# The affine part of three layer norms moved from GpSimd to VectorE, and scheduler priority round four groups of chains

## The chip, the cores and the metric

One core of one Trainium2 chip runs the whole program. A core has five engines that run beside each other, each with its own queue of instructions in program order: TensorE (PE, matrix products; PEld is its weight load), VectorE (DVE), ScalarE (ACT), GpSimd (POOL) and SyncE (SP, which here only issues DMAs). An instruction waits on semaphores until what it reads is written and what it overwrites has been read; everything behind it in the same queue waits with it. The metric is the device time of one execution in microseconds (us). Times of small kernels are written in us throughout, durations of one instruction sometimes in ns.

## The reference, cut to what matters

The reference is one step of a small diffusion backbone of two layers, for 384 tokens (128 of a context, 256 of a sample) of width 1024. Each layer has a mixing part (an mLSTM, a convolution and a retention branch, merged by gates) and a feed-forward part, and each part ends in a residual and a layer norm:

```python
def trunk_layer(x, mod, p, init, latent):
    shift1, scale1, gate1, shift2, scale2, gate2 = jnp.split(mod[:, None, :], 6, axis=-1)
    h = x * (1.0 + scale1) + shift1
    mix, new_state = mixing_sublayer(h, p, init, latent)
    x = layer_norm(DEEPNORM_ALPHA * x + gate1 * mix, p['ln1_w'], p['ln1_b'])
    h = x * (1.0 + scale2) + shift2
    a, gt = jnp.split(h @ p['ffn_w13'], 2, axis=-1)
    ff = (jax.nn.silu(gt) * a) @ p['ffn_w2']
    x = layer_norm(DEEPNORM_ALPHA * x + gate2 * ff, p['ln2_w'], p['ln2_b'])
    return x, new_state
```

The norm is `(x - mu) * rsqrt(var + eps) * w + b`. Its last two steps, times `w` and plus `b`, are called the affine part here. The next product reads `h`, a scaled and shifted norm; the affine result itself is read only by the residual after that.

## The kernel before, in words

**Products.** Everything is in fp32, and a product is made of three passes: each operand is split into a high part (a cast) and a low part (the rest), and PE adds high x high (L255), high x low and low x high (L256, L257). Weights come by DMA on SP's queue into three buffers (`wraw`), ACT casts the high part (`whi`, L205, five buffers) and DVE subtracts for the low part (`wlo`, L206, four buffers). So every weight tile passes through SP, ACT and DVE in this order before PE can use it. Activations are split likewise (`h1h`, `h1l` before a mixing part, `h2h`, `h2l` before a feed-forward part, `fAh`, `fAl` within it).

**Tokens.** The 384 tokens lie in three tiles `x0`, `x1`, `x2` of 128 tokens by 1024. A projection (`proj`) takes the output columns in two halves of 512 and the tokens t = 0, 1, 2 within each half. After each product DVE scales it by the gate (L423, `gmix`), adds it to `x` (L425 or L427) and takes statistics (L431). Behind the second half of a token stands the norm: statistics merged (L436), variance plus epsilon (`rs_ve`, L318, DVE), its power -1/2 on POOL (`rs`, L319), and `x` minus the mean times `rs` on DVE (L442, in two halves).

**From the norm to the next product.** `make_hT` transposes a token's `x` on PE (L306, two groups of four), ACT applies scale and shift with the norm's weights already folded in (`hf`, L310), DVE casts the high part (L313) and subtracts the low part (L314). It is called for token t once token t + 1 has been normed; the last call is held back into the first product of the next stage, which begins with token 0, then 1, then 2. Behind each `make_hT` stands `affine`: on POOL, in place in `x`, times `w` (L450) and plus `b` (L451), two halves each. This happens at three places: norm 1 of layer 0, norm 2 of layer 0, norm 1 of layer 1. The last norm of all works with the weights at once (L444, L445) and has no `affine`. The prediction calls the three places C, D and E; they lie at 456 to 485, 761 to 796 and 1186 to 1220 us of the span.

**What sets the order.** The code is written in the order of the products; helpers that run beside them are Python generators on a list, and `tick()` after each product advances each of them by a step (`spawn(gen, delay)` waits `delay` ticks first; `finish` runs one to its end). The mLSTM and retention heads, the gates, the convolution's taps (`cacc`, L756) and the loading of later modulation constants go this way. A scheduler then orders the instructions of each engine by dependencies, priorities and the order of the program; the queues of the trace are its result.

**Retention heads.** A head makes decay weights (`gef`), two score products, then DVE multiplies scores by decay: `rpa` (L705, L706) and `rpb` (L707), which PE reads at once in L710 and L714. `rgT` (L771) is a gate of the same branch: a product times a sigmoid `sig` from ACT (L770).

**Constants of the norms.** `ln_consts` (L414) issues eight DMAs on SP that spread gate, weight and bias rows over 128 partitions into `lnc`; they share a pool of buffers with other tiles, and SP waits in its queue where a buffer is still read.

Of the kernel before, what the change touches and what calls it, by code (L numbers as in the profile page):

```python
# [14 lines left out]
P = 128  # L15
# [25 lines left out]
        (1, 3): ((1, 3, 0, 16),), (1, 5): ((0, 3),)}  # L41
WHI = 5
# [55 lines left out]
def tile_kernel(ctx: ExitStack, tc: tile.TileContext, a: dict, o: list):  # L98
# [37 lines left out]
    rate = {"fill": 0.0, "acc": 0.0, "taps": 0.0, "tacc": 0.0}  # L136

# [161 lines left out]
    def make_hT(ha, t, S, B):  # L299

        m = 0 if t == 0 else 1
        for q in range(2):
            ps = psum()
            for j in range(4):
                f = 4 * q + j
                tr(ps[:, j * P:(j + 1) * P], x[t][:, f * P:(f + 1) * P], ident)  # L306
            hf = tmp((P, 4, P), "hf")
            for j in range(4):
                f = 4 * q + j
                act(hf[:, j, :], ps[:, j * P:(j + 1) * P], AF.Identity, bias=B[:, f, m:m + 1], scale=S[:, f, m:m + 1])  # L310
            h, l_ = ha.t[q]
            s = slice(t * P, (t + 1) * P)
            nc.vector.tensor_copy(h[:, :, s], hf)  # L313
            tt(l_[:, :, s], hf, h[:, :, s].bitcast(F32), op=ALU.subtract)  # L314
# [179 lines left out]
    def mixing(l, ha, v1, rv):  # L494
# [26 lines left out]
        def gates(ps):  # L521
# [8 lines left out]
            nc.vector.tensor_copy(natG, pt[:, 0:48].rearrange("p (t c) -> p t c", c=16))  # L530
            gv = natG.rearrange("p t (d g h) -> p t d g h", d=2, g=2)
            X = tmp((P, NT, 2, NH), "X", 1)
            nc.vector.tensor_copy(X, gv[:, :, :, 1, :])
            lf = tmp((P, NT, 2, NH), "lf", 1)
            log_sigmoid(lf.rearrange("p t d h -> p (t d h)"), X.rearrange("p t d h -> p (t d h)"), (P, 24))
            for d in range(2):
                c0 = 32 * d
                nc.vector.tensor_copy(GG[:, :, 0, c0:c0 + 4], gv[:, :, d, 0, :])
                ts_(GG[:, :, 1 + d, c0:c0 + 4], lf[:, :, d, :], -1.0, None, op0=ALU.mult)
                nc.vector.tensor_copy(GG[:, :, 1 + d, c0 + 4:c0 + 8], lf[:, :, d, :])  # L540
# [8 lines left out]
            nc.vector.tensor_copy(R, pr[:, 0:T])  # L549
            scan = nc.vector.tensor_tensor_scan  # L550
            scan(R[64:68, 0:P], R[0:4, 0:P], R[0:4, 0:P], 0.0, op0=ALU.max, op1=ALU.max)
            scan(R[64:68, P:T], R[0:4, P:T], R[0:4, P:T], m0r[0:4, :], op0=ALU.max, op1=ALU.max)
            rp = slice(P - 1, None, -1)
            rs_ = slice(T - 1, P - 1, -1)
            scan(R[96:100, rp], R[32:36, rp], R[32:36, rp], 0.0, op0=ALU.max, op1=ALU.max)
            scan(R[96:100, rs_], R[32:36, rs_], R[32:36, rs_], m0r[32:36, :], op0=ALU.max, op1=ALU.max)
            act(RM[64:128, :], R[64:128, :], AF.Copy, scale=-1.0)
            stt(RM[0:64, :], R[64:128, :], -1.0, RM[64:128, :].bitcast(F32), op0=ALU.mult, op1=ALU.subtract)
# [4 lines left out]
            nc.vector.tensor_copy(natR, pn[:, 0:T].rearrange("p (t c) -> p t c", c=P))  # L563
            rb = natR.rearrange("p t (s d c) -> p t s d c", s=2, d=2)
            tt(nm, rb[:, :, 0, :, 4:8], rb[:, :, 1, :, 0:4], op=ALU.add)
            act(enm, nm, AF.Exp, scale=-1.0)
# [30 lines left out]
        def mheads():  # L597
# [3 lines left out]
            for h in range(NH):  # L601
                b1, b2 = scores(mkT, mqT, h)
                pts, qws, kws = [], [], []
                for d in range(2):
# [4 lines left out]
                    win = tmp((P, 256), "win")  # L609
                    act(win, pm[:, P:T], AF.Exp, bias=m0b[:, d, h:h + 1])  # L610
                    dl = tmp((P, 512), "dl")
                    if d == 0:
                        segs = ((0, P, 0, 0, MF[:, 0:P]), (P, 256, P, 1, MF), (T, P, 256, 2, MF[:, 0:P]))
                    else:
                        segs = ((0, P, 0, 0, MB[:, P:256]), (P, P, P, 1, MB[:, P:256]), (256, 256, P, 2, MB))
                    for o0, n, i0, t, msk in segs:
                        stt(dl[:, o0:o0 + n], pm[:, i0:i0 + n], av[:, t:t + 1], msk, op0=ALU.add, op1=ALU.min)
                    act(dl, dl, AF.Exp)
                    kw = tmp((P, P), "kw")
                    wcol = dl[:, 127:128] if d == 0 else dl[:, 0:1]  # L620
                    act(kw, kn[:, h, :], AF.Copy, scale=wcol)
                    qw = tmp((P, 256), "qw")
                    nc.gpsimd.tensor_tensor(qw, mqT[:, h, P:T], win, op=ALU.mult)
                    if d == 0:
# [450 lines left out]
    for l in range(DEPTH):  # L1075
        mA = mixing(l, ha, v1, rv)
        while l == 0 and len(fillers) > 27:
            fill()
# [4 lines left out]
        def after1(t):  # L1083
            make_hT(h2, t, S2, B2)
            affine(t, lc)
# [59 lines left out]
```

## Time and profile before

| | |
|---|---|
| median of 3 runs | 1487.69 us (1487.66, 1487.69, 1488.17) |
| the profiled execution | 1490.92 us, span of its instructions 1488.9 us |
| PE busy | 1438.7 us, 97% of the span |
| DVE busy | 944.7 us, 63% |
| ACT busy | 576.8 us, 39% |
| POOL busy | 233.2 us, 16% |
| mean granted TensorE clock | 0.984 of full speed |

The profile counts a matmul as busy from issue to its modelled end, so 97% says that PE has nearly always something in hand, not that it streams at its peak. The span is from the first to the last instruction; 2.0 us of the profiled execution lie outside it, and that execution is 3.2 us above the median of the runs without a profile. In the rows below a number in square brackets is idle time of that engine just before the instruction, with the work that ended it.

### The profile page before, as it was taken

What the parts mean: (1) busy time and instruction counts of PE and PEld (TensorE: products, weight loads), DVE (VectorE), ACT (ScalarE), POOL (GpSimd) and SP (SyncE); (2) the same over time, 40 slices, a digit from 0 to 9 for tenths busy, and PEclk for the clock granted to TensorE, in tenths of its full rate; (3) what the DMA queues carried; (4) which work ended last, traced back from release to release, by engine and by line L of the source; (5) the groups of instructions that cost most, each with busy time, mean ns of one, the idle gap of its engine ahead of it and who ended that gap; (6) DMA issues with size and microseconds to landing.
All of it is one profiled execution on the core that took longest, in us unless ns stands there. A gap on an engine that the chain in (4) does not pass through costs nothing. (4 is left out here: it accounts for less than half of the span.)

```text
span 1488.9 us, 20492 instructions
## 1 busy us (share of the span) xinstructions
PE 1438.7 (97%) x7990; PEld 1302.5 (87%) x7990; DVE 944.7 (63%) x1755; ACT 576.8 (39%) x1026; POOL 233.2 (16%) x242
## 2 busy tenths in 40 slices
PE   6999999999998999999999999989999989999997
PEld 4799999989986888979967999989999869899996
DVE  3457688996647545354375477989975674454446
ACT  2434555332523423323243345553325243242330
POOL 1003233002214100000042023320021250000000
PEclk8999999999999999999999999999999999999999
DMA  9465352464473474645644532324434525243441
GB/s 330 159 226 173 125 185 87 154 226 158 138 259 128 142 254 131 222 155 173 212 141 122 162 118 81 118 68 124 132 108 147 169 71 202 82 155 100 142 156 42
DMA packets 131713, 226.22 MB, mean 152 GB/s; under 512 B 12552, under 2 KB 62200, under 8 KB 126496
## 3 DMA queue, kind: packets, MB, share of 16 engines
q1 hardware_dynamic: 130144, 222.78, 45.2%
q0 software_dynamic: 1472, 2.14, 0.5%
q8 instruction: 62, 1.02, 0.3%
q14 instruction: 35, 0.29, 0.1%
HBM read 221.18 MB, written 3.71 MB: 151 GB/s over the span
## 5 line engine op out<-in xcount | busy, mean ns | idle before, releaser
L205 ACT CAST whi<-wraw 128x512 fp32r<-128x512 f32 (+1 forms) x484 | 338.7, 722 | 624.5 <-PE ps L256 268.1
L206 DVE TENSOR_TENSOR wlo<-wraw,whi 128x512 fp32r<-128x512 f32 (+1 forms) x484 | 403.5, 857 | 195.4 <-PE ps L257 92.4
L255 PE MATMUL ps<-h1h,whi 128*128 128x384 f32 x896 | 306.0, 341 | 0.0
L257 PE MATMUL ps<-h1h,wlo 128*128 128x384 f32 x896 | 299.9, 335 | 0.0
L256 PE MATMUL ps<-h1l,whi 128*128 128x384 f32 x896 | 299.8, 335 | 0.0
L255 PE MATMUL ps<-h2h,whi 128*128 128x384 f32 x576 | 193.9, 337 | 0.0
L257 PE MATMUL ps<-h2h,wlo 128*128 128x384 f32 x576 | 192.6, 334 | 0.0
L256 PE MATMUL ps<-h2l,whi 128*128 128x384 f32 x576 | 192.6, 334 | 0.0
L255 PEld LDWEIGHTS ps<-h1h,whi 128*128 128x128 f32 x896 | 168.4, 188 | 13.7 <-issue 8.4
L256 PEld LDWEIGHTS ps<-h1l,whi 128*128 128x128 f32 x896 | 168.5, 188 | 0.1
L257 PEld LDWEIGHTS ps<-h1h,wlo 128*128 128x128 f32 x896 | 168.3, 188 | 0.0
L756 DVE SCALAR_TENSOR_TENSOR cacc<-u,cwt,cacc 128x399 f32<-128x399 f32 x232 | 148.6, 661 | 2.0
L255 PEld LDWEIGHTS ps<-h2h,whi 128*128 128x128 f32 x576 | 108.1, 188 | 8.5 <-issue 4.2
L256 PEld LDWEIGHTS ps<-h2l,whi 128*128 128x128 f32 x576 | 108.1, 188 | 0.2
L257 PEld LDWEIGHTS ps<-h2h,wlo 128*128 128x128 f32 x576 | 108.1, 188 | 0.0
L255 PE MATMUL ps<-whi,fAh 128*128 128x512 f32 x264 | 103.4, 392 | 0.0
L257 PE MATMUL ps<-whi,fAl 128*128 128x512 f32 x264 | 102.9, 390 | 0.0
L256 PE MATMUL ps<-wlo,fAh 128*128 128x512 f32 x264 | 102.8, 389 | 0.0
L423 DVE TENSOR_TENSOR gmix<-ps,lnc 128x512 f32<-128x512 f32 x48 | 33.1, 689 | 81.2 <-PE ps L257 81.2
L928 DVE TENSOR_TENSOR gf<-ps,sig 128x384 f32<-128x384 f32 x36 | 20.1, 558 | 91.1 <-PE ps L257 91.1
L319 POOL TENSOR_TENSOR rs<-rs_ve,half 128x1 f32<-128x1 f32 x18 | 15.4, 856 | 380.8 <-DVE rs_ve L318 380.8
L844 POOL TENSOR_TENSOR mg<-mg,sig 128x384 f32<-128x384 f32 x32 | 42.4, 1330 | 200.5 <-DVE sig L843 200.5
(303 smaller groups left out, 2194.8 us busy)
## 6 DMA issues: line engine op xcount, KB each, us to landing
wraw<-in_in_w_dram SPq DMA_DIRECT2D x64, 1024.0 KB
wada<-in_ada_w_dram SPq DMA_DIRECT2D x40, 1024.0 KB
wraw<-in_ffn_w_dram SPq DMA_DIRECT2D x76, 512.0 KB
wraw<-in_ffn_w_dram SPq DMA_DIRECT2D x28, 1024.0 KB
wraw<-in_out_w_dram SPq DMA_DIRECT2D x8, 1024.0 KB
adaq<-in_ada_w_dram SPq DMA_DIRECT2D x8, 512.0 KB
wraw<-in_mlstm_out_w_dram SPq DMA_DIRECT2D x4, 1024.0 KB
wraw<-in_ret_out_w_dram SPq DMA_DIRECT2D x4, 1024.0 KB
```

Of the source, the lines that this page charges most:

```text
L205: nc.scalar.copy(hi, src)
L206: tt(lo, src, hi.bitcast(F32), op=ALU.subtract)
L255: mm(out, sh, vh, start=(first and i == 0), stop=False)
L256: mm(out, sh, vl, start=False, stop=False)
L257: mm(out, sl, vh, start=False, stop=(last and i == n - 1))
L319: nc.gpsimd.tensor_tensor(out, ve, half[:, 0:shape[1]], op=ALU.pow)
L423: tt(g, ps, lc[0 if t == 0 else 1, hf], op=ALU.mult)
L756: stt(ac, u[:, k:k + CW], wk, ac, op0=ALU.mult, op1=ALU.add)
L844: nc.gpsimd.tensor_tensor(dst, dst, sg[j], op=ALU.add)
L928: tt(f, ps, sg[j], op=ALU.mult)
```

## The change

`affine` on POOL goes. Its 36 instructions (three places, three tokens, two halves, a product and a sum each) are issued on DVE by a generator `affines`, which is spawned behind the last `make_hT` of the place with a delay of five ticks and gives out one half (two instructions) a tick; it is run to its end before the next projection that writes `x`. Its product is held in its place in the program's order; the sum is not. Second, `urgent()` gives a higher priority to the scheduler for ACT's and DVE's part of `make_hT`, for residual and norm of the final halves, for the gates' chains, and for the chains inside the mLSTM and retention heads.

```diff
+URG = 200
+AFF = 5
+    def urgent():
+        return tc.high_priority(offset=URG)
...
@@ make_hT @@
-            hf = tmp((P, 4, P), "hf")
...
-            nc.vector.tensor_copy(h[:, :, s], hf)
-            tt(l_[:, :, s], hf, h[:, :, s].bitcast(F32), op=ALU.subtract)
+            with urgent():
+                hf = tmp((P, 4, P), "hf")
...
+                nc.vector.tensor_copy(h[:, :, s], hf)
+                tt(l_[:, :, s], hf, h[:, :, s].bitcast(F32), op=ALU.subtract)
...
-    def affine(t, lc):
-        for hf in range(2):
-            v = x[t][:, hf * 512:(hf + 1) * 512]
-            nc.gpsimd.tensor_tensor(v, v, lc[2, hf], op=ALU.mult)
-            nc.gpsimd.tensor_tensor(v, v, lc[3, hf], op=ALU.add)
+    def affines(lc):
+
+        for t in range(NT):
+            for hf in range(2):
+                v = x[t][:, hf * 512:(hf + 1) * 512]
+                tc.keep_in_program_order(tt(v, v, lc[2, hf], op=ALU.mult))
+                tt(v, v, lc[3, hf], op=ALU.add)
+                yield 0
...
@@ proj @@
-                resid(t, hf, ps, lc, first, final)
                 if final and hf == 1:
-                    norm(t, lc if after is None else None)
+                    with urgent():
+                        resid(t, hf, ps, lc, first, final)
+                        norm(t, lc if after is None else None)
+                else:
+                    resid(t, hf, ps, lc, first, final)
...
@@ rheads (mheads and gates likewise, each chain in one urgent block) @@
-                tt(pa[:, 0:P], b1[:, 0:P], ef[:, P:256], op=ALU.mult)
-                tt(pa[:, P:T], b1[:, P:T], ef[:, P:T], op=ALU.mult)
-                tt(pb, b2[:, 0:256], ef[:, 0:256], op=ALU.mult)
+                with urgent():
+                    pa = tmp((P, T), "rpa")
+                    pb = tmp((P, 256), "rpb")
+                    tt(pa[:, 0:P], b1[:, 0:P], ef[:, P:256], op=ALU.mult)
+                    tt(pa[:, P:T], b1[:, P:T], ef[:, P:T], op=ALU.mult)
+                    tt(pb, b2[:, 0:256], ef[:, 0:256], op=ALU.mult)
...
+    aff = []
     for l in range(DEPTH):
         mA = mixing(l, ha, v1, rv)
...
+        while aff:
+            finish(aff.pop())
...
         def after1(t):
             make_hT(h2, t, S2, B2)
-            affine(t, lc)
+            if t == NT - 1:
+                aff.append(spawn(affines(lc), AFF))
...
             w2 = a["ffn_w2"][l, k0 * P:(k0 + n) * P, :]
+            while aff:
+                finish(aff.pop())
...
                 def after2(t):
                     make_hT(ha, t, S1, B1)
-                    affine(t, lc2)
+                    if t == NT - 1:
+                        aff.append(spawn(affines(lc2), AFF))
```

What the scheduler makes of it, engine by engine: POOL has the same instructions as before less the 36, so that the three `rs` of a place stand one behind the other. At C and at E the order of DVE round the norm is row for row what it was. It differs in three places. (The changed kernel's line numbers are 5 to 29 higher; L459 and L460 are the affine product and sum.)

DVE in the feed-forward part of layer 0 behind place C, where the first tiles of its weights are split. Before:

```order
L206 TENSOR_TENSOR wlo_4759<-wraw_4750,whi_4758 128x512
L206 TENSOR_TENSOR wlo_4830<-wraw_4825,whi_4829 128x512
L206 TENSOR_TENSOR wlo_4836<-wraw_4825,whi_4835 128x512
L911 TENSOR_TENSOR sgB_4628<-ps_4709,sgB_4628 128x512
L206 TENSOR_TENSOR fAl_4492<-ps_4735,fAh_4491 128x4x128
L206 TENSOR_TENSOR wlo_4830<-wraw_4827,whi_4829 128x512
```

And with the change, from the same tile on (`sgB` is a product of the gated unit, `fAl` the low part of its output):

```order
L211 TENSOR_TENSOR wlo_4747<-wraw_4738,whi_4746 128x512
L459 TENSOR_TENSOR x0_77<-x0_77,lnc_4172 128x512
L211 TENSOR_TENSOR wlo_4822<-wraw_4817,whi_4821 128x512
L460 TENSOR_TENSOR x0_77<-x0_77,lnc_4173 128x512
L932 TENSOR_TENSOR sgB_4616<-ps_4697,sgB_4616 128x512
L459 TENSOR_TENSOR x0_77<-x0_77,lnc_4172 128x512
L211 TENSOR_TENSOR fAl_4484<-ps_4723,fAh_4483 128x4x128
L460 TENSOR_TENSOR x0_77<-x0_77,lnc_4173 128x512
```

The affine instructions stand singly between the splits of weights, the order of x being 0, 2, 1; the last of them stand some twenty rows further on, ahead of the first split for the next projection. It is the same behind E.

DVE at place D, from token 1's residual to its norm. Before:

```order
L423 TENSOR_TENSOR gmix_6753<-ps_6728,lnc_5057 128x512
L427 TENSOR_TENSOR x1_78<-x1_78,gmix_6753 128x512
L431 BN_STATS bn1_6633<-x1_78 128x6
L313 CAST h1h_6551<-hf_6770 128x4x128
L436 BN_AGGR mv_6757<-bn1_6633 128x2
L314 TENSOR_TENSOR h1l_6552<-hf_6770,h1h_6551 128x4x128
L318 TENSOR_SCALAR rs_ve_6760<-mv_6757 128x1
L206 TENSOR_TENSOR wlo_6870<-wraw_6867,whi_6869 128x1024
L442 TENSOR_SCALAR x1_78<-x1_78,mv_6757,rs_6759 128x512 x2
```

With the change:

```order
L430 TENSOR_TENSOR gmix_6753<-ps_6728,lnc_5057 128x512
L459 TENSOR_TENSOR x0_77<-x0_77,lnc_5057 128x512
L434 TENSOR_TENSOR x1_78<-x1_78,gmix_6753 128x512
L460 TENSOR_TENSOR x0_77<-x0_77,lnc_5058 128x512
L438 BN_STATS bn1_6633<-x1_78 128x6
L320 CAST h1h_6551<-hf_6770 128x4x128
L443 BN_AGGR mv_6757<-bn1_6633 128x2
L211 TENSOR_TENSOR wlo_6862<-wraw_6859,whi_6861 128x1024
L325 TENSOR_SCALAR rs_ve_6760<-mv_6757 128x1
L321 TENSOR_TENSOR h1l_6552<-hf_6770,h1h_6551 128x4x128
L449 TENSOR_SCALAR x1_78<-x1_78,mv_6757,rs_6759 128x512 x2
```

One affine half of token 0 has come ahead, into the middle of token 1's chain, and the split of the weights now stands ahead of `rs_ve`, not behind it. The fourth split of this place (`wlo_6876`, before `wlo_6884`) falls behind token 2's statistics and token 1's casts, and PE takes six matmuls of token 1 ahead of those that read it.

DVE in the fourth retention head of layer 1. Before:

```order
L745 TENSOR_TENSOR u_8511<-ps_8486,xc_8048 128x256
L705 TENSOR_TENSOR rpa_8892<-sc1_8887,gef_8817 128x128
L706 TENSOR_TENSOR rpa_8892<-sc1_8887,gef_8817 128x256
L771 TENSOR_TENSOR rgT_8842<-ps_8859,sig_8884 128x384
L707 TENSOR_TENSOR rpb_8893<-sc2_8888,gef_8817 128x256
```

With the change:

```order
L766 TENSOR_TENSOR u_8511<-ps_8486,xc_8048 128x256
L726 TENSOR_TENSOR rpa_8892<-sc1_8887,gef_8817 128x128
L727 TENSOR_TENSOR rpa_8892<-sc1_8887,gef_8817 128x256
L728 TENSOR_TENSOR rpb_8893<-sc2_8888,gef_8817 128x256
L792 TENSOR_TENSOR rgT_8842<-ps_8859,sig_8884 128x384
```

`rpb` and `rgT` have changed places. In the other heads the work ahead of `rpa` is the same up to one tap more or less, and the gates' small copies stand a little earlier.

On SP, `ln_consts` for norm 2 stands where it stood. Its fourth and its seventh DMA waited for POOL and now wait for DVE's affine instructions to have read the buffers; one load of weights has moved ahead of the fourth, two stand behind the eighth as before.

## Rows read from the trace of the kernel before

**Rows 1.** Waits of PE: line <- what, us in total, times, longest.

```profile
PE rvo L710 <- DVE rpa L705: 7.8, 4, 2.7
PE ps L306 <- DVE x L442: 4.8, 3, 2.4
PE ps L257 <- DVE h2l L314: 2.9, 3, 1.0
PE ps L255 <- DVE h2h L313: 2.5, 2, 1.7
PE rvo L714 <- DVE rpb L707: 2.3, 1, 2.3
PE ps L255 <- DVE h1h L313: 1.7, 1, 1.7
PE ps L257 <- DVE h1l L314: 0.5, 1, 0.5
```

**Rows 2.** Timeline of PE at place C: start us, us, instruction, [idle before].

```profile
467.83 1.11 PE L306 MATMUL ps<-cc,x 128*128 128x128 f32 x8 [1.22 <-DVE x L442]
473.73 0.50 PE L256 MATMUL ps<-wlo,h2h 128*128 128x512 f32 x1 [0.43 <-DVE wlo L206]
476.83 0.50 PE L255 MATMUL ps<-whi,h2h 128*128 128x512 f32 x1 [1.68 <-DVE h2h L313]
478.52 0.80 PE L257 MATMUL ps<-whi,h2l 128*128 128x512 f32 x1 [0.95 <-DVE h2l L314]
```

**Rows 3.** Windows: us, busy time of PE, PEld, DVE, ACT, POOL; granted PEclk.

```profile
478.52:484.60 6.08, 6.08 (x19) 5.01 (x19) 2.08 (x6) 0.51 (x2) 1.50 (x2) 0.50 0.00 0
783.70:788.40 4.70, 4.70 (x12) 3.63 (x13) 2.09 (x6) 0.00 (x0) 0.99 (x1) 0.50 0.53 145
989.80:996.60 6.80, 5.25 (x23) 5.25 (x24) 6.12 (x12) 3.89 (x9) 0.00 (x1) 0.50 0.03 9
1198.00:1201.40 3.40, 3.40 (x13) 2.89 (x12) 3.40 (x6) 2.68 (x8) 2.87 (x2) 0.50 0.15 26
```

**Rows 4.** Timeline of PE in layer 1's retention heads, and at place E.

```profile
960.29 0.49 PE L710 MATMUL rvo<-rv,rpa 128*128 128x128 f32 x2 [2.11 <-DVE rpa L705]
988.30 0.46 PE L710 MATMUL rvo<-rv,rpa 128*128 128x128 f32 x2 [1.95 <-DVE rpa L705]
991.35 0.80 PE L714 MATMUL rvo<-rv,rpb 128*128 128x128 f32 x2 [2.33 <-DVE rpb L707]
...
1197.64 1.67 PE L306 MATMUL ps<-cc,x 128*128 128x128 f32 x8 [2.40 <-DVE x L442]
```

**Rows 5.** Timeline of DVE at place C.

```profile
464.55 2.24 DVE L206 TENSOR_TENSOR wlo<-wraw,whi 128x1024 fp32r<-128x1024 f32 x1
467.23 1.00 DVE L442 TENSOR_SCALAR x<-x,mv,rs 128x512 f32<-128x512 f32 x2 [0.44 <-POOL rs L319]
468.49 1.22 DVE L206 TENSOR_TENSOR wlo<-wraw,whi 128x1024 fp32r<-128x1024 f32 x1
```

**Rows 6.** Line L427 of DVE: ns min/median/max.

```profile
L427 DVE TENSOR_TENSOR x<-x,gmix x24: 691/693/1773, 643.0 to 1481.5; 128x512 f32<-128x512 f32 x24
```

**Rows 7.** Timeline of POOL at place C.

```profile
462.53 3.17 POOL L451 TENSOR_TENSOR x<-x,lnc 128x512 f32<-128x512 f32 x2
465.67 1.53 POOL L319 TENSOR_TENSOR rs<-rs_ve,half 128x1 f32<-128x1 f32 x1
```

**Rows 8.** Timeline of ACT at places C and E: casts of weights.

```profile
462.61 1.05 ACT L205 CAST whi<-wraw 128x1024 fp32r<-128x1024 f32 x1 [0.16 <-PE ps L257]
...
1192.12 2.98 ACT L205 CAST whi<-wraw 128x1024 fp32r<-128x1024 f32 x3
```

**Rows 9.** Timeline of DVE in the fourth retention head of layer 1.

```profile
990.41 0.56 DVE L771 TENSOR_TENSOR rgT<-ps,sig 128x384 f32<-128x384 f32 x1 [1.93 <-ACT sig L770]
```

**Rows 10.** Windows: the feed-forward stretch behind place C.

```profile
490.00:520.00 30.00, 30.00 (x151) 25.34 (x150) 15.08 (x21) 12.37 (x19) 0.00 (x0) 1.00 0.48 172
```

**Rows 11.** Timeline of SP behind place C.

```profile
527.07 2.10 SPq L414 DMA_DIRECT2D lnc<-g  x4
```

More of the change, by code (lines that the diff above doesn't have):

```diff
@@ L630, in mheads @@
-                    pts.append(dl)
-                    qws.append(qw)
-                    kws.append(kw)
+                    with urgent():
+                        win = tmp((P, 256), "win")
+                        act(win, pm[:, P:T], AF.Exp, bias=m0b[:, d, h:h + 1])
+                        dl = tmp((P, 512), "dl")
+                        if d == 0:
+                            segs = ((0, P, 0, 0, MF[:, 0:P]), (P, 256, P, 1, MF), (T, P, 256, 2, MF[:, 0:P]))
+                        else:
+                            segs = ((0, P, 0, 0, MB[:, P:256]), (P, P, P, 1, MB[:, P:256]), (256, 256, P, 2, MB))
+                        for o0, n, i0, t, msk in segs:
+                            stt(dl[:, o0:o0 + n], pm[:, i0:i0 + n], av[:, t:t + 1], msk, op0=ALU.add, op1=ALU.min)
+                        act(dl, dl, AF.Exp)
+                        kw = tmp((P, P), "kw")
+                        wcol = dl[:, 127:128] if d == 0 else dl[:, 0:1]
+                        act(kw, kn[:, h, :], AF.Copy, scale=wcol)
+                        qw = tmp((P, 256), "qw")
+                        nc.gpsimd.tensor_tensor(qw, mqT[:, h, P:T], win, op=ALU.mult)
+                        if d == 0:
+                            tt(dl[:, 0:T], b1[:, 0:T], dl[:, 0:T], op=ALU.mult)
+                            tt(dl[:, T:512], b2[:, P:256], dl[:, T:512], op=ALU.mult)
+                        else:
+                            tt(dl[:, 0:256], b1[:, 0:256], dl[:, 0:256], op=ALU.mult)
+                            tt(dl[:, 256:512], b2[:, 0:256], dl[:, 256:512], op=ALU.mult)
+                        pts.append(dl)
+                        qws.append(qw)
+                        kws.append(kw)
@@ L690, in rheads @@
[L690 to L700 removed]
+                with urgent():
+                    ef, eb = tmp((P, T), "gef"), tmp((P, T), "geb")
+                    ts_(ef, dist, 0.0, lgc[0], op0=ALU.max, op1=ALU.mult)
+                    ts_(eb, dist, 0.0, lgc[1], op0=ALU.min, op1=ALU.mult)
+                    act(ef, ef, AF.Exp)
+                    act(eb, eb, AF.Exp, scale=-1.0)
+                    stt(ef, dist, 0.0, ef, op0=ALU.is_ge, op1=ALU.mult)
+                    stt(eb, dist, 0.0, eb, op0=ALU.is_le, op1=ALU.mult)
+                    nc.gpsimd.tensor_tensor(ef, ef, eb, op=ALU.add)
+                    qx, kws = [], []
+                    for d in range(2):
+                        e = tmp((P, 256), "win")
+                        act(e, ip1 if d == 0 else ip1[:, ::-1], AF.Exp, scale=lgc[d])
+                        q_ = tmp((P, 256), "qw")
+                        nc.gpsimd.tensor_tensor(q_, rqT[:, h, P:T], e, op=ALU.mult)
+                        qx.append(q_)
+                        kw = tmp((P, P), "kw")
+                        act(kw, kn[:, h, :], AF.Copy, scale=zeta[:, d, h:h + 1])
+                        kws.append(kw)
@@ L701, in rheads @@
                 yield 0
                 b1, b2 = scores(rkT, rqT, h)
-                pa = tmp((P, T), "rpa")
-                pb = tmp((P, 256), "rpb")
-                tt(pa[:, 0:P], b1[:, 0:P], ef[:, P:256], op=ALU.mult)
-                tt(pa[:, P:T], b1[:, P:T], ef[:, P:T], op=ALU.mult)
-                tt(pb, b2[:, 0:256], ef[:, 0:256], op=ALU.mult)
+                with urgent():
+                    pa = tmp((P, T), "rpa")
[3 more added lines that the diff above has]
+                    tt(pb, b2[:, 0:256], ef[:, 0:256], op=ALU.mult)
```

106 lines of the change are left out of this document (36 added, 70 removed).

## The prediction

> **What bounds the kernel now.** I read the page first: PE is busy for 97% of the span (the table above), so time can be won only where PE waits or runs at the lower clock. The second view is therefore the waits of PE [rows 1]: the reader is to see that nearly all of the larger ones end on DVE, in two families, the retention heads (`rpa`, `rpb`) and the three places C, D and E where a norm passes into the next product (`x` L442, then `h2h`, `h2l`, or `h1h`, `h1l`). The third is PE's timeline at C [rows 2]: four waits, 1.22 + 0.43 + 1.68 + 0.95 = 4.3 us, within 11 us. The fourth is the granted clock [rows 3]: behind these waits it lies at 0.50, the lower of its two levels (1.2 GHz instead of 2.4), so PE pays once for the wait and once more behind it. Last come the engines that feed PE there. At C a split of weights takes 2.24 us and shortly after, with the same shape, 1.22 [rows 5]; the long one runs beside POOL's L451 [rows 7]. A 128x512 tensor_tensor on DVE has a minimum and a median of 0.69 us, a longest of 1.77 [rows 6]. And `rs`, one number a partition, starts only where L451 ends and takes 1.53 us, while DVE stands idle for it before L442 [rows 5, 7]. So POOL's affine costs PE time though POOL is idle for 84% of the span: it slows DVE beside it and stands ahead of `rs`.
>
> **Place C, norm 1 of layer 0.** The order of DVE round the norm is the same, POOL's affine is gone. Token 1's L442 stands behind a split whose cast ends at 462.61 + 1.05 = 463.7 [rows 8], a cast that waited for PE and so does not come earlier. Split at 1.22: 464.9. `rs` is raised to its power meanwhile, since its input stands ahead of the split. So L442 starts at 464.9, not at 467.23, and its first half, which was enough for PE 0.6 us after its start, is there at 465.5; PE was ready at 467.83 - 1.22 = 466.6 [rows 2]. The wait goes with 1.1 us to spare. From L442 to the `h2l` of the last wait DVE has eleven instructions: L442 (1.0), three splits (3 x 1.22), and seven that take 0.69 at most: 9.5 us, so 474.4 at the latest, and earlier since two are short casts. PE without its waits stands there at 478.52 - 4.28 = 474.2. All four waits go: 4.3 us. Between 0 (if the slow splits have another reason) and 4.3, I take 4.3.
>
> **Place D, norm 2 of layer 0.** The waits are 4.8 - 1.22 - 2.40 = 1.2 on L442, 1.7 on `h1h`, 0.5 on `h1l` [rows 1, 2, 4], and one on a split like C's 0.4: 3.8 us. Here two affine instructions (2 x 0.69 = 1.4) have come into token 1's chain, and the split stands ahead of `rs_ve`, so that `rs` no longer runs beside it. C's arithmetic gives 1.1 us of room at L442, and the split's wait for its cast covers some of the rest, so I leave 0.2 of the wait on L442 and 0.3 on `h1l`. The fourth split falls behind six DVE instructions, some 3 us later; PE takes six matmuls ahead of its readers, 6 x 0.2 = 1.2 us (12 took 4.70 us at half the clock [rows 3]), and the splits ahead of it come earlier than before: I leave 0.7. Gain 3.8 - 1.2 = 2.6; ends 0 and 3.8.
>
> **Place E, norm 1 of layer 1.** Waits: 2.40 on L442 [rows 4], 2.5 - 1.68 = 0.8 on `h2h`, 2.9 - 0.95 = 1.9 on `h2l` [rows 1, 2], about 0.4 on a split: 5.5 us. The split ahead of L442 waits for the first of three casts that begin at 1192.12 [rows 8], so for 1193.1; with 1.22 it ends at 1194.3, then `rs_ve` and `rs` follow and L442 starts at 1195.2 to 1195.5. PE is ready at 1197.64 - 2.40 = 1195.2 and starts 0.6 behind L442: 0.9 stays. Further on DVE alone is about as long as PE at full clock; I leave another 0.6. Gain 4.0; ends 0 and 5.5.
>
> **The retention heads.** `rpa` is waited for four times, 7.8 us; what stands ahead of it on DVE is the same, so these stay (one tap of 0.7 more or less either way). In the fourth head of layer 1 `rpb` stood behind `rgT`, and that had waited 1.93 us for a sigmoid [rows 9]; PE waited 2.33 us [rows 4]. With the two exchanged `rpb` is ready half a microsecond after `rpa`, beside PE's first product. Gain 2.3. In the mLSTM heads and gates PE has no wait of this size, so their priority is worth nothing in either direction.
>
> **The clock.** Half of PE's busy time in the low windows is the price: (6.08 + 4.70 + 5.25 + 3.40) / 2 = 3.0 (C), 2.35 (D), 2.6 (fourth head), 1.7 (E) [rows 3], 9.7 in all. What PE did before: the clock stayed full after a lone wait of 2.11 at 960.29 and one of 1.22 at 467.83, and fell after 2.40 at E, after 1.95 and 2.33 together in the head, after 0.43, 1.68 and 0.95 together at C [rows 2, 4]. With the change the largest left are 0.9 (E), 0.7 (D) and the lone 1.95 (head), all under 2.11. So I take all of it but half of D's, where three small waits stay: 9.7 - 1.2 = 8.5; ends 0 and 9.7. The Trainium skill speaks against so clean a limit: its page "TensorE: Matmul & The Clock Gate", Part 1, says that the gate follows how busy PE has been, watched over a stretch that runs freely and doesn't begin with the kernel's work, so that one and the same wait may or may not cost the clock. By that rule nothing in the rows promises these 8.5 us, and the sum would be the waits alone; it is the first rival below.
>
> **What is added.** 36 instructions on DVE at 0.69 [rows 6]: 24.8 us, some 8.3 a place, most of it in the feed-forward stretch behind it. There PE is busy throughout at full clock and DVE for 15.1 of 30 us [rows 10]: there is room, since a split starts when PE frees a buffer and four buffers lie between. But a split can be held by one affine instruction (0.69) or a pair (1.4), at the places where PE was already waiting on a split by 0.4. Ends 0 and 24.8; I take 2.0, five delays of 0.4 us. The new wait on SP: DMA four and seven of the next norm's constants wait for the last affine product and sum; behind them in SP's queue stand two loads of weights. Before, the eight were issued from 527.07 on [rows 11]; DVE reaches its last affine some 7 us later by the place of these rows, and the constants are read only after the next product. The loads behind were waiting for buffers anyway. 0; ends 0 and 3.
>
> **Sum.** Waits 4.3 + 2.6 + 4.0 + 2.3 = 13.2, clock 8.5, added 2.0: 19.7 us less. Against the profiled execution (1488.9 span and 2.0 outside it) that is 1490.9 - 19.7 = 1471.2; against the median of the runs, 3.2 us lower, it is 1468.0. Which part of the 3.2 lies in these waits no view shows: I forecast 1470, with 1464 to 1474 for this case.
>
> **Rivals.**
> First: the waits go, the clock doesn't follow. For it speaks that a wait of 1.95 is left in the head and 0.9 at E; against it the lone wait of 2.11 that cost no clock. 13.2 - 2.0 = 11.2 less: 1476.5 to 1479.7, say 1478. By the rule of the Trainium skill above it would be about as likely as the forecast.
> Second: the change doesn't do what it says at the norms. The priorities move nothing at C and E, and if DVE's stretched instructions had another cause than POOL, only the head's 2.3 to 4.9 is left, less the 2.0 added: 1485 to 1488. Against it: of 24 executions of L427 half take 0.69, and the long splits lie where POOL runs.
> Third, slower: DVE becomes the bound behind C and E. Each of 18 affine halves ahead of a split holds it by 1.4 us; where PE has used up its four buffers it waits as long. All 18 cost 25 us, and with waits of that kind the clock isn't won back: 1490.9 - 13.2 + 25 = 1502 at worst. It decides from the tenth exposed half on (10 x 1.4 against 13.2), about 1492. Against it stands DVE at 50% in that stretch [rows 10].
>
> **Chances.** Forecast 0.60, first rival 0.22, second 0.11, third 0.07. A measurement of this kernel can tell about 0.2%, 3.0 us. The forecast, the first rival and nearly half of the second are faster by more: 0.87. The other half of the second is within it: 0.06. Slower 0.07. The range reaches from 1462 (every wait and all of the clock gone, nothing given back: 1487.7 - 15.9 - 9.7) over the first rival to 1481: two in ten lie outside, above it mostly.
>
> **What would show it.** In the changed kernel's profile: DVE's long instructions at C, D, E back at 0.69 and 1.22, `rs` no longer behind another instruction, L442 no longer waited for at C, and `rpb` gone from PE's waits, each right or wrong by itself; the granted clock 1.00 at C, E and in the fourth head. `rpa` should still stand with nearly 8 us. If PE's waits on `wlo` grow far over 2 us, or the clock at C still falls though the waits are gone, the sum is wrong by the one or the other.

## The result, and the profile after

The changed kernel takes 1466.78 us (median of 4 runs, 1465.80 to 1467.83) against 1487.68 (1487.65 to 1488.17): a ratio of 0.9859, 95% interval 0.9842 to 0.9876, so 20.9 us less. The profiled execution took 1465.80, its span is 1464.0. The execution profiled of the kernel before took 1490.92, so the spans of the two traces (1488.9 and 1464.0) differ by 24.9 us: before's execution was 3.2 above its median, after's 1.0 below. What is read from the two traces adds up to 24.9, what the kernel is worth is 20.9.

First the page of the kernel after, busy time by engine and the clock in 40 slices (9 is 90% or more):

```profile
PE 1424.0 (97%) x7990; PEld 1294.5 (88%) x7990; DVE 938.1 (64%) x1791; ACT 575.8 (39%) x1026; POOL 165.1 (11%) x206
...
PEclk9999999999999999999999999999999999999999
```

POOL has fallen to 11%, and PE's share has not moved, since waits and busy time at the lower clock went together. The waits of PE after, which answer to [rows 1] (line numbers moved by 5 to 21: L306 is now L311, L442 L449, L206 L211, L425 L432, L705 L726):

```profile
PE rvo L731 <- DVE rpa L726: 7.9, 4, 2.4
...
PE ps L889 <- DVE rs_ve L325: 2.2, 2, 1.2
PE rvo L731 <- ACT whi L210: 1.9, 1, 1.9
...
PE ps L889 <- DVE xn L884: 1.3, 1, 1.3
PE ps L261 <- DVE wlo L211: 1.1, 4, 0.4
```

`x` L442 (4.8), `h2l`, `h2h`, `h1h`, `h1l` and `rpb` are gone; at L731 the waits for `rpa` stand with 7.9, 7.8 before, and one of 1.9 us at the same line is put down to ACT; and L889, the norm of the convolution in layer 1, is new. DVE's timeline at place C after, to hold against [rows 5]:

```profile
458.93 0.69 DVE L432 SCALAR_TENSOR_TENSOR x<-x,gmix 128x512 f32<-128x512 f32 x1
459.65 0.69 DVE L438 BATCH_NORM_STATS2 bn<-x 128x6 f32<-128x512 f32 x1
460.26 0.41 DVE L320 CAST h2h<-hf 128x512 fp32r<-128x512 f32 x1
...
461.42 1.22 DVE L211 TENSOR_TENSOR wlo<-wraw,whi 128x1024 fp32r<-128x1024 f32 x1
463.09 1.00 DVE L449 TENSOR_SCALAR x<-x,mv,rs 128x512 f32<-128x512 f32 x2 [0.44 <-POOL rs L326]
```

The long split is back at 1.22, and L449 starts at 463.09 where L442 started at 467.23. POOL's timeline at C after, against [rows 7]:

```profile
461.61 1.44 POOL L326 TENSOR_TENSOR rs<-rs_ve,half 128x1 f32<-128x1 f32 x1 [5.58 <-DVE rs_ve L325]
```

Of POOL's work only `rs` is left there, and this one still takes 1.44 us. PE at C shows no wait. The granted clock at C, D, E and in layer 1's retention heads (columns as in [rows 3]):

```profile
457.00:484.00 27.00, 27.00 (x138) 20.82 (x137) 19.75 (x34) 17.64 (x34) 2.37 (x2) 1.00 0.42 137
754.00:785.00 31.00, 30.76 (x153) 23.59 (x153) 23.35 (x37) 18.28 (x35) 3.28 (x3) 1.00 0.51 154
1172.00:1210.00 38.00, 37.58 (x179) 30.88 (x178) 22.91 (x36) 20.09 (x38) 2.26 (x2) 1.00 0.22 69
943.00:976.00 33.00, 29.06 (x186) 28.09 (x187) 29.56 (x70) 22.99 (x36) 9.83 (x11) 1.00 0.35 103
```

It is at its upper level throughout: only 0.24 us of waiting is left at D and 0.42 at E, and in the heads three lone waits of 2.29, 1.17 and 1.95 us cost no clock in this execution. What replaces them is at the convolution norm. PE's timeline there, after:

```profile
1100.60 0.33 PE L889 MATMUL ps<-cc,xn 128*128 128x128 f32 x1 [0.96 <-DVE rs_ve L325]
1102.15 0.33 PE L889 MATMUL ps<-cc,xn 128*128 128x128 f32 x1 [1.22 <-DVE rs_ve L325]
1103.75 2.39 PE L889 MATMUL ps<-cc,xn 128*128 128x128 f32 x10 [1.27 <-DVE xn L884]
```

Three waits in a row, all for DVE. DVE's timeline there, after:

```profile
1087.21 2.11 DVE L211 TENSOR_TENSOR wlo<-wraw,whi 128x512 fp32r<-128x512 f32 x3 [6.00 <-ACT whi L210]
...
1093.77 3.81 DVE L211 TENSOR_TENSOR wlo<-wraw,whi 128x512 fp32r<-128x512 f32 x3
1097.51 1.29 DVE L879 BATCH_NORM_STATS2 hbn<-ps 128x6 f32<-128x512 f32 x2
...
1102.88 0.81 DVE L884 TENSOR_SCALAR xn<-ps,mv,rs 128x512 f32<-128x512 f32 x1 [0.73 <-POOL rs L326]
```

The norm's chain follows without a gap on splits that stand ahead of it. But these splits came late: DVE stood idle for 6.00 us, since ACT had no weights to cast. In the chain of work that ended last, followed through this stretch, the load of these weights is the longest piece:

```profile
1071.22 2.03 DVE wlo L211 x2
1073.27 13.27 DMA wraw<-in_in_w_dram
```

The load goes out once DVE has split the tiles that held its buffers, and those splits stood between the convolution's taps. It landed 13.27 us later, then ACT could cast. The same chain of DVE in the kernel before:

```profile
1114.25 1.28 DVE L858 BATCH_NORM_STATS2 hbn<-ps 128x6 f32<-128x512 f32 x2
...
1119.62 0.81 DVE L863 TENSOR_SCALAR xn<-ps,mv,rs 128x512 f32<-128x512 f32 x1 [0.73 <-POOL rs L319]
```

And its reader on PE before, which had no wait:

```profile
1120.39 1.47 PE L868 MATMUL ps<-cc,xn 128*128 128x128 f32 x12
```

DVE's chain came 16.7 us earlier (1119.62 to 1102.88), PE came into the stretch 21.4 us earlier. Most of the difference appears as three small waits, 0.96 + 1.22 + 1.27 = 3.45 us, and behind them the clock falls, so that PE pays again (a window of after, columns as above):

```profile
1103.75:1107.20 3.45, 3.45 (x15) 3.45 (x16) 2.28 (x3) 3.26 (x5) 0.00 (x0) 0.51 0.30 68
```

3.45 us of matmuls at half the clock are 1.7 more, 5.2 in all. The whole difference by place follows from setting the n-th matmul of one trace against the n-th of the other: by how much earlier PE reaches it, and where that grows. The same was done for each experiment (us gained on the trace of before, times of before's span; what is missing to the sum lies mostly in the first 320 us, where two executions of the changed kernel differ by 2.0):

| stretch | after | no priority | priority only | late on POOL | in place on DVE | no affine | POOL writes only | fewer taps |
|---|---|---|---|---|---|---|---|---|
| C 457–500 | 8.2 | 8.2 | 1.2 | 6.2 | 7.1 | 8.2 | 6.3 | 8.2 |
| D 763–800 | 7.5 | 7.3 | 0.7 | 6.4 | 6.1 | 8.1 | 6.1 | 7.5 |
| heads of layer 1, 920–1000 | 4.7 | −1.0 | 3.0 | 3.2 | 4.6 | 4.6 | −1.6 | 2.4 |
| convolution norm 1100–1125 | −6.1 | 0.0 | −6.3 | −5.9 | −6.2 | −6.1 | 0.0 | 0.0 |
| E 1180–1230 | 9.1 | 9.1 | 0.1 | 4.8 | 2.7 | 9.1 | 7.8 | 9.1 |
| whole span | 24.9 | 24.8 | −1.8 | 12.4 | 12.0 | 22.5 | 19.0 | 26.1 |

### The profile page after: what moved, and what is told of

Same layout as the page of the kernel before. It is cut to its first block, busy times and chain, and to the rows that moved or that the text cites. A ratio compares the mean times of both kernels' runs of the same rounds, so it can differ in the third digit from the quotient of the medians.

```text
span 1464.0 us, 20461 instructions
## 1 busy us (share of the span) xinstructions
PE 1424.0 (97%) x7990; PEld 1294.5 (88%) x7990; DVE 938.1 (64%) x1791; ACT 575.8 (39%) x1026; POOL 165.1 (11%) x206
## 4 chain that ended last, share of the span: by engine, by line
PE 82%; DVE 8%; DMA 5%; ACT 2%; POOL 1%; issue 1%; SPq 0%; DVEq 0%; POOLq 0%; ACTq 0%
PE ps L260 24%; PE ps L262 24%; PE ps L261 24%; DMA wraw<-in_in_w_dram 3%; PE adaps L378 3%; DVE wlo L211 2%; DVE cacc L777 2%; PE vacc L261 1%; DMA wada<-in_ada_w_dram 1%; POOL mg L865 1%; PE vacc L262 1%; PE vacc L260 1%; DMA adaq<-in_ada_w_dram 1%; ACT whi L210 1%; PE svo L666 1%
## 5 line engine op out<-in xcount | busy, mean ns | idle before, releaser
L211 DVE TENSOR_TENSOR wlo<-wraw,whi 128x512 fp32r<-128x512 f32 (+1 forms) x484 | 402.4, 853 | 195.4 <-PE ps L262 89.5
```

The source lines that it names most:

```text
L211: tt(lo, src, hi.bitcast(F32), op=ALU.subtract)
```

## Experiments

The theory: POOL's affine, by running at the norms, slows DVE and holds `rs`; with it gone from there, waits and clock at C, D and E go. The rivals: the priorities do it; or the mere later place does it, whichever engine works; or POOL's instructions harm only as a queue ahead of `rs`.

**The priorities taken out.**

```diff
     def urgent():
-        return tc.high_priority(offset=URG)
+        return nullcontext()
```

> The changed kernel without its scheduler priority: the affine part on DVE stays. Theory (POOL's leaving is what pays at the three norms, and the 5 us won in layer 1's fourth retention head are given back at the convolution's norm at 1100 us, where DVE's chain is late): 1466 to 1468 us, the changed kernel's time within 1 us; PE's waits at C, D and E together under 2 us; PE waits 2 to 2.5 us on rpb again, and on the convolution's norm under 1 us where the changed kernel waits 3.5. Rival A (the priority carries part of the gain at the norms): over 1474 us, with waits on L442, h2h and h2l back. Rival B (the head's gain is kept in the changed kernel): 1471 to 1472 us.

Measured: 1467.09 (1465.94 to 1469.22), ratio 0.9850 (0.9834 to 0.9865): the time of the whole change. Its trace tells why nothing is lost with the head's gain: the wait on `rpb` is back, and L889 stands in no row of PE's waits, of which these two answer to the question.

```profile
PE rvo L731 <- DVE rpa L726: 7.7, 4, 2.5
...
PE rvo L735 <- DVE rpb L728: 2.8, 2, 2.6
```

The head's gain and the loss at the convolution norm come and go together (4.7 and −6.1 with priority, −1.0 and 0 without). DVE's last step of that norm starts at 1102.88 with priority and at 1103.74 without: 5.7 us won in the heads brought it forward by 0.9.

**The priorities alone, the affine on POOL and in its old place.**

```diff
     def after1(t):
         make_hT(h2, t, S2, B2)
-        if t == NT - 1:
-            aff.append(spawn(affines(lc), AFF))
+        affine(t, lc)
```

> The other half alone: scheduler priority, with the affine part on POOL as before. Theory: 1486 to 1488 us, within 2 us of the kernel before; the waits at C, D and E as before (some 13 us together), rpb no longer waited for, and a new wait of 2 to 4 us at the convolution's norm of layer 1. Rival A (priority carries part of the norms' gain): under 1480 us. Rival B (the head's gain is kept): 1482 to 1483 us.

Measured: 1490.56 (1489.66 to 1492.49), ratio 1.0002 (0.9992 to 1.0012), beside 1490.07 for the kernel before on that chip. The waits of [rows 1] at C, D and E are all there again, with those at the convolution norm (here L895) added:

```profile
PE ps L311 <- DVE x L449: 4.8, 3, 2.4
...
PE ps L262 <- DVE h2l L321: 2.9, 3, 1.0
PE ps L895 <- DVE rs_ve L325: 2.2, 2, 1.2
...
PE ps L260 <- DVE h1h L320: 1.7, 1, 1.7
```

So the first rival falls: priority is worth nothing here, from the first experiment and from this one. DVE's timeline at C in this kernel, to be held against the rows after:

```profile
460.74 1.58 DVE L432 SCALAR_TENSOR_TENSOR x<-x,gmix 128x512 f32<-128x512 f32 x1
462.36 0.69 DVE L438 BATCH_NORM_STATS2 bn<-x 128x6 f32<-128x512 f32 x1
462.96 0.80 DVE L320 CAST h2h<-hf 128x512 fp32r<-128x512 f32 x1
...
465.46 2.25 DVE L211 TENSOR_TENSOR wlo<-wraw,whi 128x1024 fp32r<-128x1024 f32 x1
```

POOL's timeline over the same microseconds:

```profile
460.50 2.98 POOL L466 TENSOR_TENSOR x<-x,lnc 128x512 f32<-128x512 f32 x2 [2.66 <-PE ps L311]
463.44 3.18 POOL L467 TENSOR_TENSOR x<-x,lnc 128x512 f32<-128x512 f32 x2
```

The same four instructions take 1.58, 0.69, 0.80, 2.25 beside POOL and 0.69, 0.69, 0.41, 1.22 without it: the two with two inputs from SBUF (L432, L211) and the cast about double, the statistics, with one input, do not change.

**POOL against DVE, and in place against late.** Two kernels fill the other corners. In the first the late generator runs on POOL:

```diff
-                tc.keep_in_program_order(tt(v, v, lc[2, hf], op=ALU.mult))
-                tt(v, v, lc[3, hf], op=ALU.add)
+                tc.keep_in_program_order(nc.gpsimd.tensor_tensor(v, v, lc[2, hf], op=ALU.mult))
+                tc.keep_in_program_order(nc.gpsimd.tensor_tensor(v, v, lc[3, hf], op=ALU.add))
```

> The changed kernel with the affine part issued by the same late generator, but on POOL, both instructions held in the program's order. It tells whether it was POOL's work as such or its place beside the norm's chain. Theory (the place): C and E as in the changed kernel, waits there under 1 us; the splits of weights in the feed-forward stretch take 1.2 to 2.2 us beside POOL's affine, hidden since PE has four buffers: 1465 to 1470 us. Rival (the contention follows the work): PE waits on wlo grow by 5 us or more in the feed-forward stretches, 1473 us or more.

In the second DVE does the affine in place, behind each token's norm:

```diff
+    def affine(t, lc):
+        for hf in range(2):
+            v = x[t][:, hf * 512:(hf + 1) * 512]
+            tc.keep_in_program_order(tt(v, v, lc[2, hf], op=ALU.mult))
+            tc.keep_in_program_order(tt(v, v, lc[3, hf], op=ALU.add))
...
-            if t == NT - 1:
-                aff.append(spawn(affines(lc), AFF))
+            affine(t, lc)
```

> The changed kernel with the affine part on DVE directly behind each token's make_hT, held in the program's order, in place of the late generator: the engine without the lateness. With POOL in place (the kernel before and the one with priority alone) and POOL late (1477.6) it completes the four combinations. Theory (both count: the norm's chain must have DVE for itself): the third and fourth split of weights at C, D and E stand behind six to ten affine instructions of 0.69 us, PE waits 3 to 5 us on wlo at each place and loses the clock at some: 1476 to 1488 us. Rival (only POOL's slowing counted, order on DVE is free): 1466 to 1469 us.

| affine | in place, behind each token's norm | later |
|---|---|---|
| on POOL | 1490.56, ratio 1.0002 | 1477.60 (1475.69 to 1478.70), 0.9914 (0.9896 to 0.9932) |
| on DVE | 1478.20 (1476.93 to 1481.57), 0.9918 (0.9899 to 0.9937) | 1466.78, 0.9859 |

Either half alone gives 0.8 to 0.9%, some 12 us, both together 1.4%. The late one on POOL missed what the theory expected of it: POOL's work slows DVE wherever it runs, and eight waits on splits stand where four stand after. At C it now lies beside the norm's last step, L449, which takes 2.92 us for its two halves and 1.00 in the changed kernel. In place on DVE there is no contention, but the four affine instructions a token stand ahead of splits, and at E one split comes 3.6 us late. PE's waits in the kernel with the late generator on POOL:

```profile
PE ps L261 <- DVE wlo L211: 3.4, 8, 0.6
...
PE ps L311 <- DVE x L449: 1.7, 4, 0.7
```

`x` is waited for again too, 0.7 at the longest. PE's timeline at E in the kernel with DVE in place:

```profile
1198.18 0.50 PE L261 MATMUL ps<-wlo,h2h 128*128 128x512 f32 x1 [3.58 <-DVE wlo L211]
```

That one wait is more than half of what this kernel lacks at E (9.1 − 2.7 = 6.4 us), and behind it the clock falls.

**No affine at all.**

```diff
             if t == NT - 1:
-                aff.append(spawn(affines(lc), AFF))
+                pass
```

> The changed kernel with the affine part of the three norms left out altogether (neither on POOL nor on DVE), so the price of the 36 added DVE instructions can be read. Theory (they lie in DVE's idle time): 1465.5 to 1467.5 us, within 1 us of the changed kernel. Rival (they hold splits of weights, as the prediction's 2.0 us say): 1464 to 1465 us. Rival B (DVE is the bound behind the norms): under 1460 us.

Measured: 1468.09 (1467.46 to 1468.21), ratio 0.9846 (0.9831 to 0.9861). On the same chip the changed kernel took 1468.81 (last experiment): the 36 instructions cost 0.7 us by these medians, which is hardly clear of the spread. By place only D is better without them, by 0.6 us.

**POOL busy as long, but only writing.** In the kernel before, the affine is replaced by one small copy and 24 memsets of a spare tile per token; DVE's order is that of before.

```diff
     def affine(t, lc):
-        for hf in range(2):
-            v = x[t][:, hf * 512:(hf + 1) * 512]
-            nc.gpsimd.tensor_tensor(v, v, lc[2, hf], op=ALU.mult)
-            nc.gpsimd.tensor_tensor(v, v, lc[3, hf], op=ALU.add)
+        scr = tmp((P, 128), "scr", 1)
+        nc.gpsimd.tensor_copy(scr[:, 0:1], x[t][:, D - 1:D])
+        for _ in range(24):
+            nc.gpsimd.memset(scr, 0.0)
```

> The kernel before, with POOL's affine part replaced, at the same place of POOL's queue, by 24 memsets of a spare 128x128 tile a token (5 to 7 us, the length of the affine part; the norms' weights and biases are left out). DVE's order is that of the kernel before row for row. POOL is as long busy ahead of each rs, but reads nothing of SBUF. Theory (POOL's affine costs time since DVE's instructions take twice as long beside it): DVE's L425, L313, L314 and splits at C, D, E go back to 0.4 to 0.7 and 1.2 us, PE's waits there fall from 13 us to 5 or less, 1472 to 1480 us. Rival (what counts is that rs stands behind POOL's work): the waits stay above 8 us, over 1484 us.

Measured: 1470.92 (1469.59 to 1471.88), ratio 0.9867 (0.9844 to 0.9890), better than expected. POOL's timeline at C in it:

```profile
458.33 6.40 POOL L451 MEMSET scr<- 128x128 f32 x24
464.70 0.55 POOL L319 TENSOR_TENSOR rs<-rs_ve,half 128x1 f32<-128x1 f32 x1
466.42 3.12 POOL L449 COPY scr<-x 128x1 f32<-128x1 f32 x1 [1.18 <-DVE x L442]
```

The memsets keep POOL for 6.40 us, and `rs` runs when they end. DVE's timeline there:

```profile
459.87 0.69 DVE L425 SCALAR_TENSOR_TENSOR x<-x,gmix 128x512 f32<-128x512 f32 x1
...
462.40 1.22 DVE L206 TENSOR_TENSOR wlo<-wraw,whi 128x1024 fp32r<-128x1024 f32 x1
465.28 1.01 DVE L442 TENSOR_SCALAR x<-x,mv,rs 128x512 f32<-128x512 f32 x2 [1.66 <-POOL rs L319]
```

POOL is as busy and as far ahead of `rs`, yet DVE runs at 0.69 and 1.22. The queue's part is what is left: `rs` waits for the memsets and L442 for `rs`, 1.66 us, and each place gains 1.3 to 1.9 less than after (6.3, 6.1, 7.8 against 8.2, 7.5, 9.1), or 1.3 to 2.0 less than the kernel without any affine, which leaves out as much. The last rival has a share, the slowing of DVE the larger one. The Trainium skill ("SBUF — State Buffer", section "Who interferes with whom") says that a DVE instruction with two SBUF inputs contends with a GpSimd instruction that reads SBUF, not with one that only writes. The traces agree: 1.58 and 2.25 beside a reading POOL, 0.69 and 1.22 beside a writing one.

**What paces the convolution norm.** Layer 1's taps are cut from 31 to 23 a group.

```diff
-            dvq.extend(tap(k) for k in range(CK))
+            dvq.extend(tap(k) for k in range(CK) if l == 0 or not 0 < k <= 8)
```

> The changed kernel with 8 of the 31 convolution taps of each channel group left out in layer 1 (the branch's result is not the convolution's): 32 DVE instructions of some 0.6 us less between 930 and 1076 us. Theory (between the fourth retention head and the convolution's norm DVE is the bound, so what PE wins in the head is given back there): the waits of PE on the convolution's norm (3.5 us in the changed kernel, 5.7 us with the low clock) go, 1460 to 1462 us. Rival (the weights' DMA is late by itself, DVE only waits for it): the waits stay at 3 us or more and the time at 1465 us or more.

Measured: 1464.13 (1462.99 to 1465.36), ratio 0.9820 (0.9805 to 0.9836); 1460 to 1462 was expected. The wait at L889 is gone, so DVE's taps are what the norm waits behind. In its trace the load of weights goes out at 1067.97 instead of 1071.84, though PE is 5.0 us further behind there than in the changed kernel: the taps held the splits, and these the load. The gain is smaller than expected; in the trace the heads won only 2.4 us. Starting the norm's thread a step earlier was the repair that leaves nothing out:

```diff
         thB = spawn(conv_norm())
+        step(thB)
```

> The changed kernel with the first step of the convolution's norm (transposes, statistics, normalisation) issued before the branch that follows it, not after the first column tile of that branch. Theory (the 5.7 us that are lost at 1100 us stem from DVE's norm chain standing behind splits whose weights come late): the chain comes some 3 us earlier, PE's wait there falls from 3.5 to under 1 us and with it most of the low clock: 1461 to 1464 us. Rival (the late weights themselves bound PE there, whatever stands in the queue): the wait moves to the next split, 1466 to 1467 us.

Worse than expected: 1473.07 (1470.63 to 1474.44), ratio 0.9886 (0.9869 to 0.9904). PE's waits at that place have changed their names and grown:

```profile
PE ps L889 <- DVE xn L884: 3.8, 2, 2.5
...
PE ps L877 <- ACT sig L855: 0.8, 1, 0.8
PE ps L260 <- ACT sig L855: 0.8, 1, 0.8
```

3.8 + 0.8 + 0.8 us stand where 2.2 + 1.3 stood. Then DVE was relieved by four of its taps a layer, the first of each group given to ACT, with the affine's sum pinned as its product is; once with the priorities, once without.

```diff
                     if k == 0:
                         st["a"] = tmp((P, UW), "cacc")
-                        ts_(st["a"][:, 0:CW], u[:, 0:CW], wk, pv(l, V_CB + j, 1), op0=ALU.mult, op1=ALU.add)
+                        act(st["a"][:, 0:CW], u[:, 0:CW], AF.Identity, scale=wk, bias=pv(l, V_CB + j, 1))
```

> The changed kernel with the first tap of each channel group (a scale and a bias) on ACT, which is 40% busy, in place of DVE, 8 instructions of 0.48 us, and with the affine sum held in the program's order too, so that no affine half comes into the norm's chain at D. Theory (DVE is the bound ahead of the convolution's norm): the loss there shrinks by about 2 us, D gains 0.5: 1464 to 1466 us. Rival: ACT's casts are delayed or the order shifts elsewhere, 1467 us or more.

> The same two edits on the changed kernel without its priority. Theory: the priority's gain in the retention head is taken back at the convolution's norm, so this is within 1 us of the kernel with priority and the two edits: 1464 to 1467 us. Rival: with DVE lighter the head's gain is kept and the priority is worth 2 to 4 us: 1467 us or more here, under 1465 there.

Measured: 1469.88 (1468.50 to 1470.76), ratio 0.9858 (0.9831 to 0.9885), with −6.7 at the convolution norm: no repair. Without priorities 1466.31 (1466.12 to 1468.15), ratio 0.9840 (0.9817 to 0.9863): by their ratios not to be told from the changed kernel or from the one without priorities. The two were run on one chip and differ by 3.6 us; by place that lies in the first 320 us (−2.1 and 1.9), which nothing here explains. The second has 3.2 in the heads and −5.8 at the convolution norm although it has no priorities: the loss goes with what the heads win, whatever wins it. No version that computes the same beats them.

**The changed kernel once more**, to see what two executions share.

> The changed kernel as it is, once more, beside the three others and the kernel before on one chip: 1465.5 to 1468 us, with the trace of another execution. If the two traces differ, the difference should lie at the retention heads of layer 0 and at the loss behind them, by 1 to 2 us, and not at C, D or E.

Measured: 1468.81 (1468.17 to 1471.32), ratio 0.9856 (0.9836 to 0.9875). At C, D and E its trace gives 8.2, 7.5 and 9.1, as the first did. Layer 0's retention differs by 3.5 us, of which 2.0 are left at 320, the heads by 1.5 (3.2 instead of 4.7); the time lies 0.8 above the expected range. In the heads the clock fell twice, behind lone waits of 2.26 and 1.85 us, where the first execution kept it (PE, PEld, DVE, ACT, POOL, then the clock):

```profile
946.90:950.30 3.40, 3.40 (x18) 3.40 (x18) 3.37 (x7) 3.32 (x5) 0.00 (x0) 0.50 0.26 96
974.20:977.60 3.40, 3.40 (x18) 3.40 (x17) 1.63 (x4) 2.73 (x5) 0.00 (x0) 0.50 0.24 90
```

Terms at the norms are thus good to a tenth, terms in the heads to some 1.5 us.

## Why the prediction was right, and where not

The forecast of 1470 for a measured 1466.78, in its range and in the case given 0.60, came from a mechanism that the runs show, and from terms whose errors partly cancel; that it came within 3.2 us is in part luck.

- **Cause, right.** POOL's affine slows DVE and holds `rs`: shown by the memsets (slowing), by what those leave (queue), and by the priorities alone (1.0002). "POOL's affine costs PE time though POOL is idle" holds.
- **C, right; one step of its working wrong.** 4.3 of waits and 3.0 of clock were counted, 8.2 came. L442 was put behind a split that had to wait for the cast ending at 463.7. The split in that slot uses an earlier cast: it starts at 461.42, before the cast of [rows 8] even begins in the trace after (461.70). And `rs` is not raised "meanwhile" at no price: beside the split it takes 1.44, and L449 waits 0.44 for it. The room was larger than 1.1, so the result stood.
- **D and E, too small.** 3.8 and 5.7 counted, 7.5 and 9.1 came. The 1.2 and 1.5 us of waits left in place did not stay (0.24 and 0.42 did). And the clock's term read too little of the trace of before: the low stretch at D begins 2.1 us ahead of the window that was counted, and was then halved; E has a second one that was not counted (windows of before, columns as in [rows 3]):

```profile
781.60:788.40 6.80, 5.92 (x14) 4.13 (x15) 4.19 (x9) 0.00 (x0) 2.49 (x3) 0.50 0.54 160
...
1208.20:1211.70 3.50, 3.11 (x8) 2.32 (x8) 2.15 (x4) 0.36 (x1) 0.95 (x1) 0.51 0.45 140
```

  Half of 5.92 is 3.0 at D, and half of 3.40 + 3.11 is 3.3 at E. With waits of 3.8 − 0.24 and 5.5 − 0.42 that makes 6.5 and 8.3; 0.7 to 1.0 us at each place, C too, no row names.
- **The clock, right at the norms, but not for its limit.** At C, D and E nothing over 0.42 us is left to wait for, and both traces of the changed kernel have 1.00 there. The limit itself, that lone waits under 2.11 us cost nothing, is wrong, as the first rival had it: in the trace after a lone 2.06 in layer 0's heads, at 232.95, brought the clock to 0.50, while 2.35 at 217.43 had not, and in the second execution 2.26 and 1.85 brought it down in layer 1. The 2.6 us counted for the fourth head were thus won in the one execution; in the other half of 3.40 us there was still lost.
- **The heads, the step that failed.** 2.3 of wait and 2.6 of clock were counted as won. `rpb` is gone, and in this execution the low clock with it, 4.7 in the trace (3.2 in the other); but the step asked only what is late next inside the head ("ready half a microsecond after `rpa`"), not what paces the stretch behind it. DVE is busy for 56.99 of 60 us there after, and its chain into the convolution norm cannot come earlier by as much as PE does. 6.1 us is given back (5.2 of it in the waits and the clock above): the heads are worth less than nothing, and the run without priorities is as fast. DVE in that window after (PE, PEld, DVE, ACT, POOL, then the clock):

```profile
990.00:1050.00 60.00, 60.00 (x351) 59.89 (x350) 56.99 (x100) 19.73 (x35) 0.00 (x0) 1.00 0.40 119
```

  DVE has 3 us to spare in 60, and PE waits for nothing in the window itself. What is late there is the splits that free the weights' buffers; it appears 13.27 us of load later, at the norm, when DVE itself has been idle for 6.00.
- **Added affines, too dear.** 2.0 us were counted, about 0.6 came (by place; 0.7 by the medians on one chip, and the ratios 0.9846 against 0.9859 and 0.9856 overlap in their intervals). In the window of [rows 10] DVE went from 15.08 to 18.67 us and PE stayed at 30.00.
- **The wait on SP, right at nothing.** The eight constants go out at 524.78, earlier than the 527.07 of [rows 11], without a wait for DVE.
- **Rivals.** The first (no clock) is out at C, D and E; in the heads it holds in the second execution. The second is out for the norms. The third is out with the affine late, but not with it in place: the 3.58 us wait on a split at E in the run with DVE in place is its mechanism, but it came once, too little to decide.
- **The sum.** 19.7 forecast, 24.9 in the traces, 20.9 in the medians: C, D and E together 8.0 more than counted; the 2.0 of added work falls away, since what came of it lies in these places already; the heads 0.2 less; the convolution norm 6.1 not foreseen; and 1.5 at places that nobody counted (0.9 in the first 320 us, 0.6 behind the convolution norm). 19.7 + 8.0 + 2.0 − 0.2 − 6.1 + 1.5 = 24.9.

## What to carry to other kernels

Elementwise work that reads SBUF on POOL is not free because POOL is idle: look for the same DVE instruction with two lengths, and if the long one lies beside POOL, move the work to DVE at a place where PE does not wait for DVE. Which engine does it and when it does it count about equally here (12 us each). For every stall won, ask what paces the next stage: where that is the engine that was waited for, or a load that it releases, the stall comes back there, and can cost the clock too.

## What the runs showed of the hardware that was not expected

- Where POOL reads, it and DVE take turns. In the run with priorities alone POOL's pair ends at 463.44 + 3.18 = 466.62; the split beside it ends at 465.46 + 2.25 = 467.71, 1.09 behind. `rs` before ends at 465.67 + 1.53 = 467.20 [rows 7], 0.41 behind its split, which ended at 464.55 + 2.24 = 466.79 [rows 5]. So most of a long duration is standing until the other engine's instruction has ended; what follows is no longer than the instruction alone (1.22 for the split, 0.55 for `rs`). POOL stands too: its 18 products took 1.28 to 4.02 us in the kernel before, the longest beside a split, a subtraction and a split of DVE that kept 1.22, 0.69 and 1.22; it ended 1.1 behind them. Two inputs are not the only condition here, since the cast (0.80 against 0.41) and L449 (2.92 against 1.00), with one tensor to read, are held as well; the statistics are not. In the run with memsets one number a partition, 0.18 us of copy on POOL when alone, took 3.12 while DVE ran a split, a subtraction and a split without a gap (466.54 to 469.50), and ended 0.04 behind them; the three kept their 1.22, 0.68 and 1.22. `rs`, 0.55 alone, took 1.44 beside a split and ended 0.41 behind it. The short reader waited for the long instructions, and did not slow them.
- The length of a wait does not tell whether the clock falls. In one trace of the changed kernel 2.35, 2.29 and 1.95 us, each by itself, left it at 1.00, while 2.06 by itself and 0.96, 1.22 and 1.27 one behind the other brought it to half; in the other 2.26 and 1.85 at the same heads did too.
